# Sample stage of a hybrid trunk: half batches, a finer hand-out, and the pooled inputs ahead of their gates

## The chip, the core and the metric

The kernel runs on one core of one Trainium2 chip. The metric is the device time of one launch in microseconds (us). Before the change it is 2243.91 us, the median of three runs (2242.6 to 2245.94). TensorE is called PE in the rows (its weight loads PEld), VectorE DVE, ScalarE ACT, GpSimd POOL, SyncE SP. All DMAs that bear on the change are issued on SP's queue, which works through them in order.

## The reference

One decoder layer: 1024 prompt tokens and 8 sequences of 4 new tokens (the samples) go through one wide input projection; its columns feed a causal pooling branch and an mLSTM matrix memory; both are gated, merged and projected out. What the change touches, cut to its core:

```python
# pooling branch, group g of 4 (256 columns each), windows 2, 4, 8, 16
pooled = moving_sum(pool_in, win) / cnt - pool_in
a      = (pooled @ pool_w[g]) * pool_scale * silu(pool_z)
# mLSTM memory of the samples: 8 sequences (batches) x 4 heads, state c is 512 x 512
num   = s @ v + g * (q @ c)                   # reads the old state
c_new = decay * c + k.T @ v                   # and writes a new one
```

The old and the new state of the samples are 32 MB each: 32 matrices of 1 MB to read, update and write.

## The kernel before

Everything is float32. A large product is done as three matmuls of a split operand (`mm3`, L376 to L378: high by high, high by low, low by high). `fm` (L429 ff.) computes one 128-column tile of a projection for all 1056 tokens (1024 and 32): 8 steps over the inner dimension by three matmuls, in three chunks of 352 columns (`CW`), or in four of 264 (`CH`) for the pooled inputs.

Work is laid out in stages. The one that matters here runs from about 1357 to 1669 us: `pool_branch` does four groups g, and in each, before the change: PZ, the gate products `pool_z` (two tiles, SiLU on ACT into `sz`); PIN, the pooled inputs (two tiles; each chunk is pooled on DVE and split into `poh` and `pol`, which stand ready as the moving operand); PW, the products with `pool_w` (inner dimension 256, so two steps instead of eight, moving operand `poh`/`pol`), whose result is multiplied into `sz` and stored.

Beside it runs `sample()` (L1044), a Python generator: after each product of eight steps, `fm` calls `tick`, which lets the generator go on to its next `yield`, `RATE_S` = 1.85 steps a product on average. A step is one batch b of one head h. It makes `km` on ACT (L1128), loads the old state as one tile `ct` of 128 x 4 x 512 (1 MB, L1130, three buffers), and then issues on PE four matmuls `num<-ct` (L1132), each 32 wide, that lie on four column groups of the array, and four `kv` products of 512 columns (L1136). On DVE each `kv` is added onto the decayed state in place (L1137). Then `ct` goes out as the new state, 1 MB (L1140). A load can take a buffer only when the store of its tenant three batches before has landed. In the trace each of these four matmuls has two records, so that a whole batch reads `x8` and a half batch `x4`.

The instruction order of each engine comes from the program's order and a list scheduler at build time that keeps a model of time: it moves independent instructions ahead where it sees a wait. So the `num` and `kv` of a batch stand among the matmuls of the gate products and pooled inputs. The weights of each product are loaded by `load_w` (L388 ff., DMA at L397; split at L363 on ACT and L369 on DVE). After this stage come two more groups of merge gates, with the rest of the sample work behind them, then the down projections and the tail.

Of the kernel before, what the change touches and what calls it, by code (L numbers as in the profile page):

```python
# [11 lines left out]
F32R = mybir.dt.float32r  # L12
AF = mybir.ActivationFunctionType
ALU = mybir.AluOpType
# [4 lines left out]
P = 128  # L19
D = 1024  # L20
T = 1024
DB, DS = 8, 4
NS = DB * DS
NT = T + NS
H, DH = 4, 512
M = H * DH
KT = D // P
L = 128
NCH = T // L
CW = NT // 3  # L30
# [7 lines left out]
O_PIN, O_PZ, O_Q, O_K = 0, D, 2 * D, 2 * D + M  # L38
# [5 lines left out]
O_GB = O_GA + D  # L44


RATE_A, RATE_S = 16.0, 1.85
HT = T // 2
SH = NS // 2
HH = HT + SH  # L50
# [3 lines left out]
class Block:  # L54
# [10 lines left out]
    def __init__(self, tr, c0):  # L65
        self.tr, self.c0 = tr, c0
        self.w = {}
        self.saved = {}
        self.raw = [[], []]
        self.begin()  # L70
# [264 lines left out]
class Trunk:  # L335
    def __init__(self, ctx, nc, tc, I, O):
        self.ctx, self.nc, self.tc, self.I, self.O = ctx, nc, tc, I, O
        self.n = 0
        self.bg = None


    def pool(self, name, side="left"):
# [87 lines left out]
    def fm(self, w, f, mov, consume, cw=CW):  # L430

        kt = len(w)
        for j in range(NT // cw):
            ps = self.mmps()
            for k in range(kt):
                wh, wl = w[k][:2]
                mh, ml = mov[k]
                s = slice(j * cw, (j + 1) * cw)
                self.mm3(ps[:, :cw], wh[:, f * P:(f + 1) * P], wl[:, f * P:(f + 1) * P], mh[:, s], ml[:, s],
                         k == 0, k == kt - 1)  # L440
            consume(j, ps)
        if kt == KT:
            self.tick()

    def feed(self, gen, rate):

        self.bg, self.rate, self.acc = gen, rate, 0.0

    def tick(self):
        if self.bg is None:  # L450
            return
        self.acc += self.rate
        while self.acc >= 1.0 and self.bg is not None:
            self.acc -= 1.0
            if next(self.bg, None) is None:
                self.bg = None
# [587 lines left out]
    def sample(self):  # L1044
        nc, I, O = self.nc, self.I, self.O
        a = self.sp
# [3 lines left out]
        ps = self.miscps()  # L1050
        for h in range(H):
            for d in range(4):
                nc.tensor.matmul(ps[32 * h:32 * h + 32, :NS], lhsT=ks[:, h * 4 + d, :], rhs=qs[:, h * 4 + d, :],
                                 start=d == 0, stop=d == 3)
        pb = self.t(a, [P, P], "pb")
        nc.gpsimd.memset(pb, 0.0)
        for h in range(H):
            s = slice(32 * h, 32 * h + 32)
            nc.vector.scalar_tensor_tensor(out=pb[s, s], in0=ps[s, :NS], scalar=KSC, in1=self.DS[s, :], op0=ALU.mult,
                                           op1=ALU.mult)  # L1060
# [3 lines left out]
        ps = self.miscps()  # L1064
# [7 lines left out]
        for h in range(H):  # L1072
            s = slice(h * 4, h * 4 + 4)
# [7 lines left out]
                                    in1=nS[:, :, :, h].unsqueeze(3).to_broadcast([P, 4, DB, DS]), op=ALU.mult)  # L1081
            for d in range(4):
                nc.tensor.matmul(den[32 * h:32 * h + 32, 0:1], lhsT=qn[:, d, :], rhs=self.ones, start=d == 0,
                                 stop=False)
# [10 lines left out]
        ps = self.miscps()  # L1095
# [7 lines left out]
        num = self.t(self.ps, [P, 2, 512], "num")  # L1103
        qm = self.t(a, [P, 132 * DB], "qm")
        nc.gpsimd.memset(qm, 0.0)
        for h in range(H):

            vf = self.t(a, [P, DH], "voz", bufs=3)[:96]
            for g in range(3):
                nc.sync.dma_start(vf[32 * g:32 * g + 32], self.vSD[h])  # L1110
            vst = self.t(a, [96, DH], "vst", F32R, bufs=1)
            self.hi(vst, vf)
            self.lo(vst[64:96], vf[64:96], vst[64:96])
            kst = self.t(a, [96, DH], "kst", F32R, bufs=1)
            ps = self.miscps()
            for d in range(4):
                nc.tensor.transpose(ps[:NS, d * P:(d + 1) * P], ks[:, h * 4 + d, :], self.ident)
            w = self.wcS[:, h:h + 1]
            self.hi(kst[0:32], ps[:NS, :], w)
            self.lo(kst[32:64], ps[:NS, :], kst[0:32], w)  # L1120
            nc.scalar.activation(kst[64:96], kst[0:32].bitcast(F32), AF.Copy)

            nc.vector.tensor_copy(qm.rearrange("p (b r) -> p b r", r=132)[:, :, 0:P]
                                  .rearrange("p b (d x) -> p b d x", d=4)[:, :, :, 0:DS],
                                  qg[:, h * 4:h * 4 + 4].rearrange("p d (b t) -> p b d t", t=DS))
            for b in range(DB):
                km = self.t(a, [96, DH], "km", F32R, bufs=1)
                nc.scalar.activation(km, kst.bitcast(F32), AF.Identity, scale=self.bcol[:96, b:b + 1])  # L1128
                ct = self.t(a, [P, 4, DH], "ct", bufs=3)
                nc.sync.dma_start(ct, I["state_mlstm_C"][b, h].rearrange("(d p) e -> p d e", p=P))  # L1130
                for d in range(4):
                    nc.tensor.matmul(num[32 * d:32 * d + 32, 0, :], lhsT=qm[:, b * P + d * NS:b * P + (d + 1) * NS], rhs=ct[:, d, :],  # L1132
                                     start=b == 0, stop=b == DB - 1)
                for d in range(4):
                    kv = self.t(self.ps, [P, 512], "kv", bufs=2)
                    nc.tensor.matmul(kv, lhsT=km[:, d * P:(d + 1) * P], rhs=vst, start=True, stop=True)  # L1136
                    nc.vector.scalar_tensor_tensor(out=ct[:, d, :], in0=ct[:, d, :],  # L1137
                                                   scalar=self.dec[:, h * DB + b, 1:2], in1=kv,
                                                   op0=ALU.mult, op1=ALU.add)
                nc.sync.dma_start(O["new_C_sample"][b, h].rearrange("(d p) e -> p d e", p=P), ct)  # L1140
                yield True
            nsb = self.t(a, [P, DH], "voz", bufs=3)
            nc.scalar.activation(nsb, num[:, 0, :], AF.Copy)
            nc.tensor.matmul(num[32 * h:32 * h + 32, 1, :], lhsT=self.sel, rhs=nsb, start=True, stop=False)
        vo = []
        for src in (self.vSD, self.oSD, self.zSD):
            x = self.t(a, [P, DH], "voz", bufs=3)
            nc.sync.dma_start(x, src.rearrange("h t e -> (h t) e"))
            vo.append(x)
        nc.tensor.matmul(num[:, 1, :], lhsT=pb, rhs=vo[0], start=False, stop=True)  # L1150
        hc = self.t(a, [P, DH], "shc")
        nc.vector.scalar_tensor_tensor(out=hc, in0=num[:, 1, :], scalar=dn, in1=vo[1], op0=ALU.mult, op1=ALU.mult)
        ss = self.t(a, [P, 1], "sss")
        nc.scalar.activation(vo[1], hc, AF.Square, accum_out=ss)
        r = self.rstd(a, ss, DH)
        nc.vector.scalar_tensor_tensor(out=hc, in0=hc, scalar=r, in1=vo[2], op0=ALU.mult, op1=ALU.mult)
        ps = self.miscps()
        for d in range(4):
            nc.tensor.transpose(ps[:, d * P:(d + 1) * P], hc[:, d * P:(d + 1) * P], self.ident)
# [3 lines left out]
    def pool_branch(self):  # L1163
        nc, I, O = self.nc, self.I, self.O
        a = self.pp
# [6 lines left out]
        for g in range(4):  # L1172
            win = 2 ** (g + 1)
            h1 = self.t(a, [DB * PH, 256], "ph1")
            nc.sync.dma_start(h1, hist[:, g * 256:(g + 1) * 256])
            w = self.load_w(I["w_in"][:, O_PZ + g * 256:O_PZ + (g + 1) * 256], 256)
            sz = []
            for f in range(2):
                z = self.t(a, [P, NT], "sz", bufs=2)

                def ev(j, ps, z=z):
                    s = slice(j * CW, (j + 1) * CW)
                    nc.scalar.activation(z[:, s], ps[:, :CW], AF.Silu)
                self.fm(w, f, self.hmov, ev)
                sz.append(z)
            w = self.load_w(I["w_in"][:, O_PIN + g * 256:O_PIN + (g + 1) * 256], 256)
            pooled = []
            for f in range(2):
# [6 lines left out]
                def ev(j, ps, f=f, ft=ft, ph=ph, pl=pl, prev=prev):  # L1195
# [45 lines left out]
                    self.hi(ph[:, c], po)  # L1241
                    self.lo(pl[:, c], po, ph[:, c])
                self.fm(w, f, self.hmov, ev, CH)
            w = self.load_w(I["pool_w"][g], 256)
            for f in range(2):
                ft = g * 2 + f
# [7 lines left out]
        for f0 in range(0, KT, 4):  # L1254
            ps = self.miscps()
# [4 lines left out]
            s = slice(f0 * P, (f0 + 4) * P)  # L1260
# [251 lines left out]
    def run(self):  # L1512
# [9 lines left out]
        d = self.dp  # L1522
# [57 lines left out]
        def rest():  # L1580
            self.rate = 1.6
            yield from gates
            _a.close()
            self.atp, _at = self.pool("attn", "right")
            self.attn_setup()
            self.rate = RATE_A
            yield from self.attn()
            _at.close()
            self.sp, st = self.pool("sample", "right")
            _s.append(st)  # L1590
            self.rate = RATE_S
            yield from self.sample()
        self.feed(rest(), 1.6)
        self.merge_gates(range(6))
        while not _s:
# [26 lines left out]
        for st in (_l, _f, _w, _c2, _c, _ps):  # L1622
# [4 lines left out]
           state_mlstm_C=(DB, H, DH, DH), state_mlstm_n=(DB, H, DH), state_mlstm_m=(DB, H), p_prompt=(T, PLE),  # L1627
# [20 lines left out]
```

## Time and profile before

| | |
|---|---|
| median of three runs | 2243.91 us |
| the profiled execution | 2243.27 us |
| its span | 2241.5 us (1.77 lie outside it) |
| PE busy in the span | 2154.4 us, 96% |
| DVE, ACT, POOL busy | 57%, 40%, 5% |
| chain that ended last | PE 87%, DMA 6%, DVE 3%, ACT 2% |
| mean granted TensorE clock | 0.986 of 2.4 GHz |

The rows of this kernel are read so: a matmul's length in a timeline includes the pipeline's latency, so the rate is the step from the start of one matmul to the start of the next; an instruction's wait stands in brackets, with the one that ended it. A window row gives a stretch, its length, the busy time and count of PE, PEld, DVE, ACT and POOL, the granted clock as a share of 2.4 GHz, the mean share of 16 DMA engines and GB/s.

### The profile page before, as it was taken

What the parts mean: (1) busy time and instruction counts of PE and PEld (TensorE: products, weight loads), DVE (VectorE), ACT (ScalarE), POOL (GpSimd) and SP (SyncE); (2) the same over time, 40 slices, a digit from 0 to 9 for tenths busy, and PEclk for the clock granted to TensorE, in tenths of its full rate; (3) what the DMA queues carried; (4) which work ended last, traced back from release to release, by engine and by line L of the source; (5) the groups of instructions that cost most, each with busy time, mean ns of one, the idle gap of its engine ahead of it and who ended that gap; (6) DMA issues with size and microseconds to landing.
All of it is one profiled execution on the core that took longest, in us unless ns stands there. A gap on an engine that the chain in (4) does not pass through costs nothing.

```text
span 2241.5 us, 40008 instructions
## 1 busy us (share of the span) xinstructions
PE 2154.4 (96%) x16311; PEld 2045.7 (91%) x16311; DVE 1267.6 (57%) x2184; ACT 903.5 (40%) x1796; POOL 120.2 (5%) x335
## 2 busy tenths in 40 slices
PE   4999999999999999899999899999999999999998
PEld 3899999999999999899999887778778999999998
DVE  7756485556745575536556674575573243543645
ACT  5535454444544453544333342232233331213443
POOL 1100000000100000000000000000000000000000
PEclk8999999999999999999999999999989999999999
DMA  3233323333233321574655645877775343323112
GB/s 129 86 107 120 102 91 110 94 107 116 85 109 110 111 88 41 164 266 143 203 163 177 195 143 168 293 267 252 255 267 171 117 128 110 101 98 111 53 48 83
DMA packets 238600, 312.70 MB, mean 140 GB/s; under 512 B 13994, under 2 KB 170066, under 8 KB 238416
## 3 DMA queue, kind: packets, MB, share of 16 engines
q1 hardware_dynamic: 238416, 310.15, 42.6%
q8 instruction: 128, 2.10, 0.4%
q14 instruction: 56, 0.46, 0.1%
HBM read 200.01 MB, written 110.45 MB: 139 GB/s over the span
## 4 chain that ended last, share of the span: by engine, by line
PE 87%; DMA 6%; DVE 3%; ACT 2%; issue 1%; SPq 1%; POOL 0%; DVEq 0%; POOLq 0%; ACTq 0%
PE mm L215 21%; PE mm L157 15%; PE mm L376 12%; PE mm L378 12%; PE mm L377 12%; PE num L1132 2%; PE misc L917 1%; PE num L376 1%; PE num L377 1%; PE kv L1136 1%; PE num L378 1%; DMA o<-oD 1%; PE kv L376 1%; DMA ct<-state_mlstm_C 1%; PE kv L377 1%; PE kv L378 1%
## 5 line engine op out<-in xcount | busy, mean ns | idle before, releaser
L369 DVE TENSOR_TENSOR wlo<-wraw,whi 128x1024 fp32r<-128x1024 f32 (+1 forms) x220 | 238.4, 1085 | 220.9 <-ACT whi L363 215.5
L363 ACT ACTIVATE whi<-wraw 128x1024 fp32r<-128x1024 f32 (+1 forms) x220 | 209.2, 951 | 348.7 <-PE mm L215 103.4
L376 PE MATMUL mm<-hh,whi 128*128 128x352 f32 (+1 forms) x832 | 264.7, 318 | 12.4 <-ACT sz L1275 6.6
L378 PE MATMUL mm<-hh,wlo 128*128 128x352 f32 (+1 forms) x832 | 262.2, 316 | 0.3 <-DVE wlo L369 0.3
L377 PE MATMUL mm<-hl,whi 128*128 128x352 f32 (+1 forms) x832 | 261.5, 314 | 0.0
L215 PE MATMUL mm<-whi,hl 128*128 128x256 f32 x768 | 216.0, 281 | 0.0
L215 PE MATMUL mm<-wlo,hh 128*128 128x256 f32 x768 | 216.0, 281 | 0.0
L215 PE MATMUL mm<-whi,hh 128*128 128x256 f32 x768 | 214.6, 279 | 0.0
L376 PEld LDWEIGHTS mm<-hh,whi 128*128 128x128 f32 x832 | 158.3, 190 | 25.6 <-ACT sz L1275 8.2
L378 PEld LDWEIGHTS mm<-hh,wlo 128*128 128x128 f32 x832 | 158.2, 190 | 6.8 <-issue 5.0
L377 PEld LDWEIGHTS mm<-hl,whi 128*128 128x128 f32 x832 | 158.7, 191 | 5.7 <-issue 4.4
L157 PE MATMUL mm<-hh,whi 128*128 128x264 f32 x512 | 149.9, 293 | 3.4 <-DVE s L624 2.4
L317 DVE SCALAR_TENSOR_TENSOR z<-z,vcols,z 128x556 f32<-128x556 f32 x192 | 146.7, 793 | 9.5 <-ACT z L315 7.9
L157 PE MATMUL mm<-hl,whi 128*128 128x264 f32 x512 | 147.3, 288 | 0.6 <-DVE hl L371 0.4
L157 PE MATMUL mm<-hh,wlo 128*128 128x264 f32 x512 | 146.7, 286 | 0.0
L215 PEld LDWEIGHTS mm<-whi,hh 128*128 128x128 f32 x768 | 144.7, 188 | 0.0
L215 PEld LDWEIGHTS mm<-whi,hl 128*128 128x128 f32 x768 | 144.6, 188 | 0.0
L215 PEld LDWEIGHTS mm<-wlo,hh 128*128 128x128 f32 x768 | 144.3, 188 | 0.2
L1137 DVE SCALAR_TENSOR_TENSOR ct<-ct,dec,kv 128x512 f32<-128x512 f32 x128 | 93.2, 742 | 73.9 <-PE kv L1136 67.0
L378 PE MATMUL mm<-mvhB,wlo 128*128 128x352 f32 x384 | 123.0, 322 | 0.0
L377 PE MATMUL mm<-mvlB,whi 128*128 128x352 f32 x384 | 122.7, 321 | 0.0
L376 PE MATMUL mm<-mvhB,whi 128*128 128x352 f32 x384 | 121.6, 323 | 0.0
(438 smaller groups left out, 6060.2 us busy)
## 6 DMA issues: line engine op xcount, KB each, us to landing
wraw<-w_in SPq DMA_DIRECT2D x112, 512.0 KB
ct<-state_mlstm_C SPq DMA_DIRECT2D x32, 1024.0 KB
new_C_sample<-ct SPq DMA_DIRECT2D x32, 1024.0 KB
qkD<-z SPq DMA_DIRECT2D x64, 256.0 KB
qk<-qkD SPq DMA_DIRECT2D x16, 1024.0 KB
sgD<-sz SPq DMA_DIRECT2D x16, 528.0 KB
sg<-sgD SPq DMA_DIRECT2D x16, 528.0 KB
vD<-z SPq DMA_DIRECT2D x32, 256.0 KB
```

Source lines behind the costliest of these rows:

```text
L157: self.tr.nc.tensor.matmul(ps[:, j, :CH], lhsT=st[:, k], rhs=mv[k][:, c], start=start and k == 0 and n == 0, stop=stop and k == 3 and n == ...
L215: self.tr.nc.tensor.matmul(ps[:, t // 2, t % 2 * 256:t % 2 * 256 + 256], lhsT=st[k][:, c], rhs=mv[:, k], start=start and t % 2 == 0 and k ...
L317: nc.vector.scalar_tensor_tensor(out=acc, in0=z[:, o:o + tot], scalar=wc(o), in1=acc, op0=ALU.mult, op1=ALU.add)
L363: self.nc.scalar.activation(out, in_, AF.Copy)
L369: self.nc.vector.tensor_tensor(out=out, in0=in_, in1=hi.bitcast(F32), op=ALU.subtract)
L376: mm(ps, lhsT=sh, rhs=mh, start=start, stop=False)
L377: mm(ps, lhsT=sh, rhs=ml, start=False, stop=False)
L378: mm(ps, lhsT=sl, rhs=mh, start=False, stop=stop)
L917: nc.tensor.matmul(out, lhsT=qk[:, 4 + d, i * L:(i + 1) * L], rhs=qk[:, d, i * L:], start=d == 0, stop=d == 3)
L1132: nc.tensor.matmul(num[32 * d:32 * d + 32, 0, :], lhsT=qm[:, b * P + d * NS:b * P + (d + 1) * NS], rhs=ct[:, d, :], start=b == 0, stop=b = ...
L1136: nc.tensor.matmul(kv, lhsT=km[:, d * P:(d + 1) * P], rhs=vst, start=True, stop=True)
L1137: nc.vector.scalar_tensor_tensor(out=ct[:, d, :], in0=ct[:, d, :], scalar=self.dec[:, h * DB + b, 1:2], in1=kv, op0=ALU.mult, op1=ALU.add)
```

## The change

The memory of a batch is held as two half tiles of 128 x 2 x 512 (512 KB), seven buffers instead of three of 1 MB; each half has its own load, its own store and its own `yield`, so that `sample()` has 64 steps in the batches instead of 32 and three more near its end. `RATE_S` doubles, and in this stage `tick` is called after every chunk of a product with the chunk's share of the rate (a third, or a quarter) instead of once a product. `km` has two buffers. In `pool_branch`, the products PIN with the pooling stand ahead of PZ.

```diff
-RATE_A, RATE_S = 16.0, 1.85
+RATE_A, RATE_S = 16.0, 3.7
@@ fm
             consume(j, ps)
-        if kt == KT:
-            self.tick()
+            if kt == KT and self.fine:
+                self.tick(cw / NT)
+        if kt == KT and not self.fine:
+            self.tick(1.0)
@@ feed, tick
-        self.bg, self.rate, self.acc = gen, rate, 0.0
+        self.bg, self.rate, self.acc, self.fine = gen, rate, 0.0, False
-        self.acc += self.rate
+        self.acc += self.rate * part
@@ sample
-                km = self.t(a, [96, DH], "km", F32R, bufs=1)
+                km = self.t(a, [96, DH], "km", F32R, bufs=2)
                 nc.scalar.activation(km, kst.bitcast(F32), AF.Identity, scale=self.bcol[:96, b:b + 1])
-                ct = self.t(a, [P, 4, DH], "ct", bufs=3)
-                nc.sync.dma_start(ct, I["state_mlstm_C"][b, h].rearrange("(d p) e -> p d e", p=P))
+                ct = []
+                for i in range(2):
+                    c = self.t(a, [P, 2, DH], "ct", bufs=7)
+                    nc.sync.dma_start(c, I["state_mlstm_C"][b, h, i * 2 * P:(i + 1) * 2 * P]
+                                      .rearrange("(d p) e -> p d e", p=P))
+                    ct.append(c)
                 for d in range(4):
-                    nc.tensor.matmul(num[32 * d:32 * d + 32, 0, :], lhsT=qm[...], rhs=ct[:, d, :],
-                                     start=b == 0, stop=b == DB - 1)
-                for d in range(4):
-                    kv = self.t(self.ps, [P, 512], "kv", bufs=2)
...
-                nc.sync.dma_start(O["new_C_sample"][b, h].rearrange("(d p) e -> p d e", p=P), ct)
-                yield True
+                    nc.tensor.matmul(num[32 * d:32 * d + 32, 0, :], lhsT=qm[...],
+                                     rhs=ct[d // 2][:, d % 2], start=b == 0, stop=b == DB - 1)
+                for i, c in enumerate(ct):
+                    for d in range(2):
+                        kv = self.t(self.ps, [P, 512], "kv", bufs=2)
...
+                    nc.sync.dma_start(O["new_C_sample"][b, h, i * 2 * P:(i + 1) * 2 * P]
+                                      .rearrange("(d p) e -> p d e", p=P), c)
+                    yield True
@@ pool_branch, each group
             nc.sync.dma_start(h1, hist[:, g * 256:(g + 1) * 256])
-            w = self.load_w(I["w_in"][:, O_PZ + ...], 256)       # PZ: sz, ten lines
...
             w = self.load_w(I["w_in"][:, O_PIN + ...], 256)
...
                 self.fm(w, f, self.hmov, ev, CH)
+            w = self.load_w(I["w_in"][:, O_PZ + ...], 256)       # the same ten lines
...
             w = self.load_w(I["pool_w"][g], 256)
@@ run, rest
-            self.rate = RATE_S
+            self.rate, self.fine = RATE_S, True
```

What the instruction order makes of it, at three places. The numbers behind a name are buffer numbers; lines of the changed file lie from 1 to 13 below those of before (`num` L1132 there is L1139, `kv` L1136 is L1144, the load L1130 is L1135, the store L1140 is L1149, `mm3` L377 to L379).

PE before, in the second half of the stage: a batch among the pooled inputs' products.

```order
L378 MATMUL mm_16533<-hh_135,wlo_16405 128x264
L376 MATMUL mm_16533<-hh_135,whi_16410 128x264
L1132 MATMUL num_15377<-ct_16383,qm_15378 32x512 x4
L377 MATMUL mm_16533<-hl_136,whi_16410 128x264
L378 MATMUL mm_16533<-hh_135,wlo_16411 128x264
L376 MATMUL mm_16533<-hh_135,whi_16410 128x264
L1136 MATMUL kv_16374<-vst_16226,km_16360 128x512
L377 MATMUL mm_16533<-hl_136,whi_16410 128x264
L378 MATMUL mm_16533<-hh_135,wlo_16411 128x264
```

PE after, early in the stage: a batch whose two halves lie apart, among gate products.

```order
L1144 MATMUL kv_15776<-vst_15384,km_15763 128x512
L1139 MATMUL num_15377<-ct_15945,qm_15378 32x512 x2
L1144 MATMUL kv_15821<-vst_15384,km_15763 128x512
L377 MATMUL mm_15968<-hh_135,whi_15830 128x352
L378 MATMUL mm_15968<-hl_136,whi_15830 128x352
L379 MATMUL mm_15968<-hh_135,wlo_15831 128x352
L377 MATMUL mm_15968<-hh_135,whi_15830 128x352
L378 MATMUL mm_15968<-hl_136,whi_15830 128x352
L379 MATMUL mm_15968<-hh_135,wlo_15831 128x352
L1139 MATMUL num_15377<-ct_15947,qm_15378 32x512 x2
```

The four `num` products of a batch stood together; now the two of each half stand with other matmuls between them in many places. Over the whole order, the `num` products form 40 uninterrupted runs before and 53 after; one of the 53 holds the products of two batches, seven in all. The number of `num` and `kv` products is the same, 128 each.

SP before, at the start of the stage: the DMA queue's stores and loads.

```order
L1140 DMA new_C_sample<-ct_15399 128x4x512
L1130 DMA ct_15647<-state_mlstm_C 128x4x512
L1140 DMA new_C_sample<-ct_15526 128x4x512
L1130 DMA ct_15834<-state_mlstm_C 128x4x512
L1140 DMA new_C_sample<-ct_15626 128x4x512
L1130 DMA ct_15855<-state_mlstm_C 128x4x512
L1140 DMA new_C_sample<-ct_15647 128x4x512
```

SP after, at the same place.

```order
L1149 DMA new_C_sample<-ct_15399 128x2x512
L1135 DMA ct_15767<-state_mlstm_C 128x2x512
L1188 DMA ph_2143_16143<-state_pool 120x256
L1149 DMA new_C_sample<-ct_15401 128x2x512
L1135 DMA ct_15869<-state_mlstm_C 128x2x512
L1149 DMA new_C_sample<-ct_15563 128x2x512
L398 DMA wraw_16145<-w_in 128x4x256
L1135 DMA ct_15871<-state_mlstm_C 128x2x512
L398 DMA wraw_16151<-w_in 128x4x256
L1149 DMA new_C_sample<-ct_15565 128x2x512
L1149 DMA new_C_sample<-ct_15667 128x2x512
L1135 DMA ct_15945<-state_mlstm_C 128x2x512
```

Each load stands behind the store that frees its buffer, as before; there are twice as many pairs, each of half the size, and SP issues 817 DMAs in all instead of 751.

PE before, where the last group's pooled inputs end.

```order
L377 MATMUL mm_18243<-hl_136,whi_17888 128x264
L378 MATMUL mm_18243<-hh_135,wlo_17889 128x264
L1209 MATMUL misc_18271<-ident_112,ph_2405_17625 128x120
L1132 MATMUL num_15377<-ct_18292,qm_15378 32x512 x4
L1257 MATMUL misc_18388<-ident_112,np_2022_15430 47x128 x2
L376 MATMUL mm_18338<-poh_17892,whi_18334 128x352
L377 MATMUL mm_18338<-pol_17893,whi_18334 128x352
L378 MATMUL mm_18338<-poh_17892,wlo_18335 128x352
```

PE after, where the last group's gate products end.

```order
L378 MATMUL mm_18372<-hl_136,whi_18164 128x352
L379 MATMUL mm_18372<-hh_135,wlo_18165 128x352
L1144 MATMUL kv_18368<-vst_17917,km_18322 128x512
L1139 MATMUL num_15377<-ct_18400,qm_15378 32x512 x2
L1139 MATMUL num_15377<-ct_18402,qm_15378 32x512 x2
L377 MATMUL mm_18428<-poh_17701,whi_18424 128x352
L378 MATMUL mm_18428<-pol_17702,whi_18424 128x352
L379 MATMUL mm_18428<-poh_17701,wlo_18425 128x352
```

Before, the products with `pool_w` follow straight on the last pooled inputs that they read; after, the 144 matmuls of the gate products stand between. From the merge gates behind this stage on, PE's order is the same (3602 rows).

## Rows read from the trace of the kernel before

**Rows 1.** Windows: stretch, length, busy us per engine, clock, DMA share, GB/s.

```profile
1357.40:1669.40 312.00, 299.48 (x1903) 240.51 (x1904) 190.99 (x393) 87.11 (x173) 14.95 (x55) 0.97 0.72 252
1360.00:1371.00 11.00, 8.47 (x54) 5.19 (x52) 4.03 (x17) 1.10 (x2) 0.00 (x0) 0.84 0.88 304
1415.00:1427.00 12.00, 10.19 (x59) 6.49 (x57) 10.81 (x22) 2.27 (x6) 0.33 (x2) 1.00 1.04 366
1490.00:1502.00 12.00, 9.85 (x54) 6.21 (x53) 8.58 (x16) 3.43 (x7) 1.52 (x3) 0.86 0.73 263
1570.00:1580.00 10.00, 7.99 (x46) 5.76 (x45) 9.46 (x20) 2.18 (x4) 0.30 (x2) 1.00 0.87 316
1645.20:1669.40 24.20, 20.35 (x87) 12.32 (x86) 18.97 (x38) 6.22 (x12) 0.59 (x3) 0.72 0.75 241
```

**Rows 2.** Groups on PE in 1357.4 to 1669.4: count, busy, mean ns, idle before.

```profile
L376 PE MATMUL mm<-hh,whi 128*128 128x264 f32 x256 | 73.7, 288 | 0.0
...
L376 PE MATMUL mm<-hh,whi 128*128 128x352 f32 x177 | 58.2, 329 | 1.0 <-ACT sz L1183 1.0
...
L1136 PE MATMUL kv<-vst,km 96*128 96x512 f32 x126 | 51.1, 435 | 1.7 <-ACT km L1128 1.0 <-DVE ct L1137 0.5
L1132 PE MATMUL num<-ct,qm 128*32 128x512 f32 x248 | 43.9, 647 | 9.7 <-DMA ct<-state_mlstm_C 7.2 <-DVE nn L1089 2.5
L376 PE MATMUL mm<-poh,whi 128*128 128x352 f32 x48 | 17.6, 379 | 0.8 <-DVE sz L1250 0.3 <-ACT poh L363 0.3
```

**Rows 3.** Timeline of PE: start, length, instruction; a product of 512 among 264.

```profile
1386.34 0.40 PE L1136 MATMUL kv<-vst,km 96*128 96x512 f32 x1
1386.58 0.29 PE L376 MATMUL mm<-hh,whi 128*128 128x264 f32 x1
1386.70 0.28 PE L377 MATMUL mm<-hl,whi 128*128 128x264 f32 x1
```

**Rows 4.** Timeline of PE: a whole batch of num between products.

```profile
1383.00 0.32 PE L377 MATMUL mm<-hl,whi 128*128 128x352 f32 x1
1383.16 0.32 PE L378 MATMUL mm<-hh,wlo 128*128 128x352 f32 x1
1383.41 1.07 PE L1132 MATMUL num<-ct,qm 128*32 128x512 f32 x8
1384.41 0.39 PE L376 MATMUL mm<-hh,whi 128*128 128x264 f32 x1
1384.64 0.28 PE L377 MATMUL mm<-hl,whi 128*128 128x264 f32 x1
```

**Rows 5.** Timeline of PE: num that waited (bracket: idle before, its releaser).

```profile
1497.00 1.93 PE L1132 MATMUL num<-ct,qm 128*32 128x512 f32 x8 [2.13 <-DMA ct<-state_mlstm_C]
...
1658.80 1.93 PE L1132 MATMUL num<-ct,qm 128*32 128x512 f32 x8 [2.58 <-DMA ct<-state_mlstm_C]
```

**Rows 6.** Chain of waits, in time: start, length, piece.

```profile
1359.08 1.95 DMA voz<-vSD
...
1413.42 4.65 DMA new_C_sample<-ct
1418.10 7.28 DMA ct<-state_mlstm_C
...
1445.88 0.98 PE num L1132 x4
...
1739.64 4.23 DMA draw<-hcD
```

**Rows 7.** Waits of the DMA queue SP, 1350 to 1700: sum, times, longest.

```profile
SPq L1130 <- DMA new_C_sample<-ct: 94.1, 26, 6.1
...
SPq L397 <- DVE wlo L369: 19.6, 14, 5.6
```

**Rows 8.** Timeline of the queue SP: a store and the load behind it.

```profile
1388.40 0.38 SPq L1140 DMA_DIRECT2D new_C_sample<-ct  x1
1392.95 0.37 SPq L1130 DMA_DIRECT2D ct<-state_mlstm_C  x1
```

More of the change, by code (lines that the diff above doesn't have):

```diff
@@ L339, in __init__ @@
         self.bg = None
+        self.fine = False
     def pool(self, name, side="left"):
@@ L441, in fm, with tick @@
             consume(j, ps)
-        if kt == KT:
-            self.tick()
+            if kt == KT and self.fine:
+                self.tick(cw / NT)
+        if kt == KT and not self.fine:
+            self.tick(1.0)
     def feed(self, gen, rate):
-        self.bg, self.rate, self.acc = gen, rate, 0.0
-    def tick(self):
+        self.bg, self.rate, self.acc, self.fine = gen, rate, 0.0, False
+    def tick(self, part):
         if self.bg is None:
             return
-        self.acc += self.rate
+        self.acc += self.rate * part
         while self.acc >= 1.0 and self.bg is not None:
@@ L1126, in sample @@
             for b in range(DB):
-                km = self.t(a, [96, DH], "km", F32R, bufs=1)
+                km = self.t(a, [96, DH], "km", F32R, bufs=2)
                 nc.scalar.activation(km, kst.bitcast(F32), AF.Identity, scale=self.bcol[:96, b:b + 1])
-                ct = self.t(a, [P, 4, DH], "ct", bufs=3)
-                nc.sync.dma_start(ct, I["state_mlstm_C"][b, h].rearrange("(d p) e -> p d e", p=P))
-                for d in range(4):
-                    nc.tensor.matmul(num[32 * d:32 * d + 32, 0, :], lhsT=qm[:, b * P + d * NS:b * P + (d + 1) * NS], rhs=ct[:, d, :],
-                                     start=b == 0, stop=b == DB - 1)
@@ L1134, in sample @@
-                for d in range(4):
-                    kv = self.t(self.ps, [P, 512], "kv", bufs=2)
[L1136 to L1139, printed above, removed]
-                nc.sync.dma_start(O["new_C_sample"][b, h].rearrange("(d p) e -> p d e", p=P), ct)
@@ L1141, in sample @@
-                yield True
+                ct = []
[4 more added lines that the diff above has]
+                    ct.append(c)
+                for d in range(4):
+                    nc.tensor.matmul(num[32 * d:32 * d + 32, 0, :], lhsT=qm[:, b * P + d * NS:b * P + (d + 1) * NS],
+                                     rhs=ct[d // 2][:, d % 2], start=b == 0, stop=b == DB - 1)
@@ new lines, in sample @@
+                for i, c in enumerate(ct):
+                    for d in range(2):
+                        kv = self.t(self.ps, [P, 512], "kv", bufs=2)
+                        nc.tensor.matmul(kv, lhsT=km[:, (2 * i + d) * P:(2 * i + d + 1) * P], rhs=vst, start=True,
+                                         stop=True)
+                        nc.vector.scalar_tensor_tensor(out=c[:, d], in0=c[:, d],
+                                                       scalar=self.dec[:, h * DB + b, 1:2], in1=kv,
+                                                       op0=ALU.mult, op1=ALU.add)
+                    nc.sync.dma_start(O["new_C_sample"][b, h, i * 2 * P:(i + 1) * 2 * P]
+                                      .rearrange("(d p) e -> p d e", p=P), c)
+                    yield True
@@ L1149, in sample @@
             vo.append(x)
+        yield True
         nc.tensor.matmul(num[:, 1, :], lhsT=pb, rhs=vo[0], start=False, stop=True)
@@ L1152, in sample @@
         nc.vector.scalar_tensor_tensor(out=hc, in0=num[:, 1, :], scalar=dn, in1=vo[1], op0=ALU.mult, op1=ALU.mult)
+        yield True
         ss = self.t(a, [P, 1], "sss")
@@ L1156, in sample @@
         nc.vector.scalar_tensor_tensor(out=hc, in0=hc, scalar=r, in1=vo[2], op0=ALU.mult, op1=ALU.mult)
+        yield True
         ps = self.miscps()
@@ L1175, in pool_branch @@
             nc.sync.dma_start(h1, hist[:, g * 256:(g + 1) * 256])
[L1176 to L1185, printed above, removed]
             w = self.load_w(I["w_in"][:, O_PIN + g * 256:O_PIN + (g + 1) * 256], 256)
@@ L1243, in pool_branch, with ev @@
                 self.fm(w, f, self.hmov, ev, CH)
+            w = self.load_w(I["w_in"][:, O_PZ + g * 256:O_PZ + (g + 1) * 256], 256)
+            sz = []
+            for f in range(2):
+                z = self.t(a, [P, NT], "sz", bufs=2)
+                def ev(j, ps, z=z):
+                    s = slice(j * CW, (j + 1) * CW)
+                    nc.scalar.activation(z[:, s], ps[:, :CW], AF.Silu)
+                self.fm(w, f, self.hmov, ev)
+                sz.append(z)
             w = self.load_w(I["pool_w"][g], 256)
```

## The prediction

> **What bounds the kernel now.** I read the page first: PE is busy for 96% of the span and carries the chain that ended last, so time can come only from PE's own work, from its clock, or from the few per cent in which it waits. Then I read windows, because the change touches one stage. That stage lasts 312.0 us, from 1357.4 to 1669.4, and PE is busy for 299.5 of them, DVE for 191, with the DMA engines at a share of 0.72 and 252 GB/s [rows 1]. PE's order behind it is the same after the change, so the stage is the whole case.
>
> How much of the 312 is work? Rates are steps between starts. A matmul of 264 columns takes 0.12 us and one of 512 (`kv`) 0.24 [rows 3]; one of 352 takes 0.16, and a batch's four `num` products take 1.00 together, with 0.23 instead of 0.12 until the second matmul behind them, so 1.11 for the run [rows 4]. Counts: 256 x 3 of 264 columns, (177 + 176 + 176) of the gates and 48 x 3 = 144 of `pool_w` at 352, 126 `kv`, and 248 records of `num`, which are 31 batches [rows 2]; these stand in 39 runs there (40 in the whole order). So 768 x 0.12 = 92.2, 673 x 0.16 = 107.7, 126 x 0.24 = 30.2, 39 x 1.11 = 43.3, and about 8 (an estimate) for small transposes and selections: 281. The other 31 us are loss.
>
> Where are they? Five windows hold 22.6 of them [rows 1]. Idle: 11 - 8.47 = 2.5 at the stage's start, 1.8 at 1415, 2.15 at 1490, 2.0 at 1570, 3.85 at the end, together 12.3; that is nearly all idle time of the stage (312.0 - 299.5 = 12.5). Clock: the granted clock is 0.84, 0.86 and 0.72 in three of them, so PE ran part of the time at 1.2 GHz, the lower level, after it had idled; that costs 0.16 x 11 + 0.14 x 12 + 0.28 x 24.2 = 10.3. A batch of `num` that waited 2.13 or 2.58 us for its state and then took 1.93 instead of 1.07 shows both at once [rows 5]. The chain says what these waits are: store of a state tile 4.65 us, and behind it the load into the same buffer 7.28 us [rows 6]; with three buffers the load cannot start before the store three batches back has landed, and the queue itself stands 94.1 us at such loads [rows 7]. The remaining 8.4 us are scattered.
>
> **The change part by part.**
>
> Split `num` products. They run four side by side on column groups. Two of them cost as much as four: a run of `x4`, half a batch, is 0.98 us on PE [rows 6], against 1.00 for the whole [rows 4]. The order after the change has 53 runs, of which one is long enough for two passes, so 54 passes instead of 40. Cost: 14 x (1.00 + 0.11) = 15.5 us. The bounds: at nothing for the 0.11, 14 x 0.98 = 13.7; and below, if the halves that stand near each other still overlap, 0, which the `x4` row speaks against, as it was measured in just such a place. I take 15.5. The `kv` products may be cut into more pieces at no cost, since a single one among other matmuls already goes at its 0.24 [rows 3].
>
> Halves and seven buffers. A buffer is freed and filled again in smaller pieces. In the order before, the shortest distances of PE work from a tile's last `kv` to the first `num` of its next tenant are (by the rates above) 8.0, 9.4, 9.8 and 10.2 us, and then 11.6; just those four waited, so the refill needs about 4.65 + 7.28 = 11.9 [rows 6]. After, the four shortest are 8.4, 9.2, 9.7 and 10.0, the next 11.1, the median 17.3 against 14.4. So the distances grow little; what counts is how long half a refill takes. The trace has no 512 KB state transfer. Bounds: no saving, 11.9, which would leave four waits of 1.9 to 3.5 us; half, 6.0, no wait. Between lie a 512 KB load with 4.23 us and a 64 KB one (`voz`, a copy of V's rows) with 1.95 [rows 6]; a line from 64 KB at 1.95 to 1 MB at 4.65 passes 512 KB at 3.2. Store and load together are then 6.4 to 8.5, and 9.7 with something for the crowd on the DMA engines (1.04 share at 1415, [rows 1]). I take 9, so waits of 0 to 0.6 and some 1.2 us in the middle three places, where 5.95 idle + 1.7 clock = 7.7 stood.
>
> Finer ticks, twice the rate. The pace of the sample work is the same, its grain is finer: 0.93 to 1.23 steps a chunk. This costs nothing on PE beyond the split above. At the start the first batch still waits for the stage's first load (idle 2.5, clock 1.8); I keep 2.5 of this 4.3, as a half tile lands sooner.
>
> PIN ahead of PZ. No instruction is added; the DMAs of two weight loads change places on SP's queue. The `pool_w` products get 144 x 0.16 = 23 us of gate products between them and the DVE pooling that they read. The end of the stage, where idle 3.85 and clock 6.8 stand, is relieved: I keep 2 of these 10.65. What this uncovers is the `sz` buffers of the next group, which are read by the `pool_w` products and stored before the next PZ; the next PIN now lies between, so they are free in time. `km` with two buffers takes out the 1.0 us that `kv` waited for `km`; `sz` waits 1.0 at the stage's first gate product, and `pool_w` 0.8 on DVE and ACT [rows 2]. With their surroundings I take 3 of the 8.4 scattered and 1.0 for the first gate product. Bounds for the two together: 0 and 9.4.
>
> Sum: of 22.6, kept 2.5 + 1.2 + 2 = 5.7, so won 16.9, + 3 + 1.0 = 20.9, less 15.5: 5.4 faster. Against the profiled execution of 2243.27 (0.64 below the median) that is 2237.9, so **2238 us**.
>
> **The rivals.**
>
> B, no difference. The waits are halved and not removed, because the distances grow so little: of 16.9 won only 8.5, + 4 - 15.5 = 3 slower, 2246. For it: the shortest distance after the change, 8.4, is no longer than 8.0 before. Against it: the median grows by 3 us.
>
> C, slower: the queue SP becomes the bound. One DMA queue in order, and behind each store the load that needs its buffer: before, a store issued at 1388.40 holds the load until 1392.95, so 4.55, + 0.37 for the load [rows 8]. If a half's store lands in 4.23 like the 512 KB row [rows 6], 64 pairs need 64 x (4.23 + 0.37) = 294; some 60 other transfers of the stage at 0.37 add 22, and half of the 19.6 us in which the queue waits for weight buffers [rows 7] add 10: 326 against a stage of 312 - 5 = 307. Then the time is 2238 + 19 = 2257. It decides from a landing of (307 - 32) / 64 - 0.37 = 3.9 us on. At 3.2 the same sum is 64 x 3.57 + 32 = 260, and the queue is not the bound. For it: the only 512 KB row. Against it: the 1.95 of the small one, and that the DMA engines are not full.
>
> The Trainium skill bears on this in "DMA: Bandwidth & Descriptors", section "Anatomy of one DMA": in its fit a transfer pays about 2.0 us of fixed time and its bytes at 436 GB/s on top, so halving a transfer halves only the second part. It is a rule that speaks against this change, fitted to another queue's path than SP's. By it 1 MB takes 4.4 (the trace: 4.65) and 512 KB 3.2 (the trace has 4.23 for another tensor); two halves 6.4 where one whole was 4.4. By the fit C would stay away, and by the row it would come.
>
> D, faster by more: two halves run at another price than the `x4` row, or mostly overlap, so that splitting costs next to nothing: 2243.3 - 20.9 = 2222. For it nothing but the lack of a row with two products of different halves a few matmuls apart.
>
> **How the numbers follow.** Forecast 0.55, with its own range of 2230 to 2246: the lower end with 9.4 instead of 4.0 for the scattered loss and 13.7 for the split, the upper one with 5 us more of waits left and none of the scattered won. B 0.18, C 0.17, D 0.10. The range over all is 2224 to 2254: it takes in B, most of D and the milder half of C. A measurement here can tell 0.2%, some 4.5 us, from no change; so faster means below 2239.4 and slower above 2248.4. Of the forecast's 0.55 some 0.40 lie below 2239.4, with D's 0.10: 0.50. Same: 0.15 of the forecast and 0.12 of B: 0.27. Slower: C's 0.17 and 0.06 of B: 0.23.
>
> **What would show it.** After the change, `num` in the timeline as `x4` near 0.98 each and more PE time in its group, if the first term is right; a run of them below 0.7 refutes it. Around 1415, 1490 and 1570 no wait on `ct` and a granted clock of 1.00; PE waits on `ct` in every group instead would speak for B, or, with SP's store-to-load steps above 4.3 us and the stage near 325, for C. `pool_w` products that wait for DVE would refute the term of the order. The stage should last about 307 us. The prediction is wrong as a whole if the stage changes by less than 2 us or grows.

## The result, and the profile after

The change makes the kernel slower: 2260.81 us (median of four runs, 2257.83 to 2263.29) against 2244.77 for the kernel before in the same rounds, a ratio of 1.0073 with a 95% interval of 1.0058 to 1.0088. The profiled execution took 2263.29 us, 20.0 more than the one before the change. Most of the time is lost in the one stage that the change edits: the last `pool_w` product starts 15.7 us later than before (1684.9 against 1669.2), and from there to PE's last matmul it takes 567.6 us instead of 563.3.

The windows of PE in the changed kernel (columns as in [rows 1]) show the stage from its first product to the end of its last, and three stretches with waits:

```profile
1357.20:1685.30 328.10, 313.54 (x1908) 245.74 (x1909) 192.21 (x387) 88.22 (x176) 13.81 (x55) 0.97 0.72 240
1425.00:1437.00 12.00, 8.72 (x39) 5.73 (x39) 5.98 (x8) 3.68 (x5) 0.00 (x0) 0.88 0.70 227
1592.00:1604.00 12.00, 9.36 (x49) 6.00 (x48) 8.42 (x13) 3.42 (x5) 0.00 (x0) 0.89 1.02 354
1655.00:1680.00 25.00, 19.48 (x100) 13.33 (x98) 8.40 (x11) 5.45 (x8) 0.00 (x0) 0.86 0.69 207
```

The stage takes 328.1 us instead of 312.0. PE is busy for 14 us more, and idle for 14.6 instead of 12.5: the idle time that was to go is still there. It has moved, and the granted clock is low again, 0.86 to 0.89 of 2.4 GHz in these three stretches. They hold 11.4 us of idle time and 6.3 of lost clock (one less the granted share, times the length). The groups on PE (the answer to [rows 2]):

```profile
L1139 PE MATMUL num<-ct,qm 128*32 128x512 f32 x256 | 59.0, 623 | 12.8 <-DMA ct<-state_mlstm_C 12.7
L1144 PE MATMUL kv<-vst,km 96*128 96x512 f32 x122 | 50.2, 422 | 1.2 <-DVE ct L1146 1.2
```

`num` costs 59.0 us for 256 records; before it was 43.9 for 248, so 45.3 for 256. The 13.7 more are 14 passes at 0.98. Its wait for `ct` is 12.7 us, where before it was 7.2 and 2.5 behind the start's small work.

The chain of waits (start, length, piece) shows the end of the last group. Before the change a store and the load behind it stood in the chain once, at 1413 [rows 6]; now stores follow each other, each released by the load issue between them:

```profile
1651.31 5.04 DMA new_C_sample<-ct
1656.38 0.38 SPq L1135
1656.85 4.96 DMA new_C_sample<-ct
1661.87 0.38 SPq L1135
1662.34 5.07 DMA new_C_sample<-ct
1667.43 0.38 SPq L1135
1667.87 5.00 DMA new_C_sample<-ct
1672.88 3.94 DMA ct<-state_mlstm_C
```

This is a lock step of the DMA queue. A store lands after 5.0 us, only then the load behind it is issued (0.38), and at once the next store, which is long due; the load has only 0.45 us to itself before the store is in flight beside it. One half takes 5.5 us, so a batch 11. Before, the stores of three batches were issued at 1388.40, 1396.79 and 1404.79, about 8.2 us a batch. PE is busy for about 9.8 us a batch (313.5 / 32): the queue kept ahead of PE then, and now is slower than PE wherever the lock step holds. That is so in stretches and not throughout: PE waits for `ct` six times, 12.7 us in all. SP's timeline has 857 DMAs against 793 before the change (not 817 against 751): 32 more loads and 32 more stores. SP's timeline shows what a half costs otherwise; first a store with no load issued in the 17 us before it, then one 0.47 us behind a load:

```profile
1379.58 0.38 SPq L1149 DMA_DIRECT2D new_C_sample<-ct  x1
1382.37 0.38 SPq L1135 DMA_DIRECT2D ct<-state_mlstm_C  x1
```

```profile
1650.84 0.38 SPq L1135 DMA_DIRECT2D ct<-state_mlstm_C  x1
1651.31 0.42 SPq L1149 DMA_DIRECT2D new_C_sample<-ct  x1
1656.38 0.38 SPq L1135 DMA_DIRECT2D ct<-state_mlstm_C  x1
```

Alone, a half has landed after 2.79 us (1379.58 to 1382.37), behind a load after 5.07. Of the 39 places in the changed kernel where a load comes right behind a store, 22 have another load less than 1.5 us ahead of the store; in 15 of these the trace names that store as what ended the load's wait, at a median of 5.06 us. That is more than the 4.2 us that the stores of a whole megabyte at 1396.79 and 1404.79 took in the kernel before, where the last load had been issued 3.8 us ahead.

### The profile page after: what moved, and what is told of

Its sections match the earlier page's. It is cut to its first block, busy times and chain, and to the rows that moved or that the text cites. A ratio compares the mean times of both kernels' runs of the same rounds, so it can differ in the third digit from the quotient of the medians.

```text
span 2261.6 us, 40109 instructions
## 1 busy us (share of the span) xinstructions
PE 2169.4 (96%) x16311; PEld 2052.4 (91%) x16311; DVE 1271.7 (56%) x2184; ACT 903.1 (40%) x1796; POOL 119.3 (5%) x335
## 4 chain that ended last, share of the span: by engine, by line
PE 87%; DMA 6%; DVE 3%; ACT 2%; issue 1%; SPq 0%; POOL 0%; DVEq 0%; POOLq 0%; ACTq 0%
PE mm L215 21%; PE mm L157 14%; PE mm L377 12%; PE mm L378 12%; PE mm L379 12%; DMA new_C_sample<-ct 2%; PE num L1139 2%; PE misc L920 2%; PE num L377 1%; PE num L378 1%; PE num L379 1%; PE kv L377 1%; PE kv L1144 1%; PE kv L378 1%; PE kv L379 1%; PE misc L703 1%
## 5 line engine op out<-in xcount | busy, mean ns | idle before, releaser
L377 PE MATMUL mm<-hh,whi 128*128 128x352 f32 (+1 forms) x832 | 266.1, 320 | 14.1 <-ACT sz L1288 8.7
L379 PE MATMUL mm<-hh,wlo 128*128 128x352 f32 (+1 forms) x832 | 262.7, 316 | 2.1 <-DVE wlo L370 2.1
L377 PEld LDWEIGHTS mm<-hh,whi 128*128 128x128 f32 x832 | 159.5, 192 | 32.9 <-ACT sz L1288 11.0
L379 PEld LDWEIGHTS mm<-hh,wlo 128*128 128x128 f32 x832 | 159.6, 192 | 5.4 <-DVE wlo L370 2.4
L379 PE MATMUL mm<-mvhB,wlo 128*128 128x352 f32 x384 | 123.3, 322 | 0.0
L377 PE MATMUL mm<-mvhB,whi 128*128 128x352 f32 x384 | 122.4, 325 | 0.2
```

Source lines behind the costliest of these rows:

```text
L377: mm(ps, lhsT=sh, rhs=mh, start=start, stop=False)
L379: mm(ps, lhsT=sl, rhs=mh, start=False, stop=stop)
```

## The experiments

Two theories were to be told apart. **Split:** a pass of `num` costs the same whether it holds two products or four, and the half tiles make more passes. **Queue:** the halves put twice as many store and load pairs into SP's queue, each of which holds up the one behind it. The rivals: the new order of the pooled inputs, the finer hand-out, the second `km` buffer. All ratios are against the kernel before on the same chip, with 95% intervals; a pass is an uninterrupted run of up to four `num` products on PE, and passes are counted in the instruction order.

**Order alone.** The kernel before with the block of the gate products (PZ) put behind that of the pooled inputs (PIN).

```diff
-            w = self.load_w(I["w_in"][:, O_PZ + ...], 256)      # PZ, ahead of PIN
...
+            w = self.load_w(I["w_in"][:, O_PZ + ...], 256)      # PZ, behind PIN
```

> The kernel before with one edit, the pooled inputs ahead of the gates; whole 1 MB tiles, 40 passes of num. If the loss of the change lies in the halves (queue or split), this one has none of it and wins the waits at the stage's end: 2236 to 2242 us. If the new order itself costs time (pooled inputs meeting the first batches, weight loads in other places), it is slower than before: 2248 or more.

0.9996 (0.9983 to 1.0009): no difference, so neither a win nor a loss of the order alone shows. `num` waits 4.8 us for `ct`, against 7.2 before.

**Halves alone.** The kernel before with half tiles in seven buffers, one step a batch.

```diff
-                ct = self.t(a, [P, 4, DH], "ct", bufs=3)
+                for i in range(2):
+                    c = self.t(a, [P, 2, DH], "ct", bufs=7)
...
```

> The kernel before with the two half tiles, seven buffers, and nothing else: one step a batch, a tick a product, the old order. 48 passes of num instead of 40. Theory queue and split together: a half's store still takes about 5 us to land and its load stands behind it, and 8 passes add 8 to 9 us: 2252 to 2262. Theory split alone (halves refill faster than whole tiles, waits go): 2244 + 9 - 10 = 2243. Theory queue alone (splitting free): 2246 to 2252, with the waits of num on ct at 10 us or more.

1.0089 (1.0076 to 1.0103), as slow as the whole change, without the new order, the finer hand-out and the second `km` buffer. PE's waits (sum, times, longest):

```profile
PE num L1136 <- DMA ct<-state_mlstm_C: 19.2, 13, 2.6
```

The waits did not go, which speaks against the split alone, and the time is above what the queue alone was to cost. So with 8 passes more, both losses are there.

**Whole tiles.** All of the change but the halves and the finer hand-out. The edit is shown against the changed kernel.

```diff
-RATE_A, RATE_S = 16.0, 3.7
+RATE_A, RATE_S = 16.0, 1.85
@@ fm
-            if kt == KT and self.fine:
-                self.tick(cw / NT)
-        if kt == KT and not self.fine:
-            self.tick(1.0)
+        if kt == KT:
+            self.tick()
@@ sample
-                    c = self.t(a, [P, 2, DH], "ct", bufs=7)
...
+                ct = self.t(a, [P, 4, DH], "ct", bufs=3)
```

> The changed kernel with whole 1 MB tiles in three buffers again and a rate of 1.85, so that a step is a batch; fine ticks, two km buffers and the new order stay. 38 passes of num. If the halves are what costs: 2232 to 2242. If the finer hand-out or the order costs, it stays above 2250.

0.9950 (0.9934 to 0.9965), 2232.31 us: faster than both kernels. PE's waits:

```profile
PE num L1132 <- DMA ct<-state_mlstm_C: 1.3, 2, 0.8
```

The expectation counts the finer hand-out (the fine ticks) among what stays, but this run's kernel calls `tick` once a product, like the kernel before. So it takes out the halves and the finer hand-out together, and what it has beyond the kernel before is the new order with two `km` buffers. No run has whole tiles with the finer hand-out, and its part is not shown here: in the instruction order it makes a difference, 41 passes of `num` instead of 38. That the halves cost without it, the run before this one shows.

**Stores on GpSimd's queue.** The changed kernel with one word changed.

```diff
-                    nc.sync.dma_start(O["new_C_sample"][b, h, i * 2 * P:(i + 1) * 2 * P]
+                    nc.gpsimd.dma_start(O["new_C_sample"][b, h, i * 2 * P:(i + 1) * 2 * P]
```

> The changed kernel with the half stores issued on GpSimd's queue, so that no store stands behind a load that waits; 60 passes of num by the scheduler's order, 6 more than the changed kernel. Theory queue: the 12.7 us of waits of num on ct and the low clock behind them (about 4) go: with the 6 passes (6 us) 2250 us. Theory split alone: nothing gained, 2261 + 6 = 2267. If a split costs nothing: 2242 or less.

1.0034 (1.0022 to 1.0047). The waits are all but gone, and the six more passes (60) stand in PE's groups:

```profile
PE num L1139 <- DMA ct<-state_mlstm_C: 2.0, 2, 1.1
```

```profile
L1139 PE MATMUL num<-ct,qm 128*32 128x512 f32 x256 | 63.4, 604 | 2.1 <-DMA ct<-state_mlstm_C 2.0
```

**Joined, and joined with stores on GpSimd's queue.** The changed kernel with the products of a batch in another sequence, which leaves 44 passes; then the same with the edit of the run before, 42 passes.

```diff
-                for d in range(4):
+                for d in (2, 0, 3, 1):
                     nc.tensor.matmul(num[32 * d:32 * d + 32, 0, :], ...
```

> The changed kernel with the four num products of a batch issued in the order 2, 0, 3, 1 (each needs the same data as before), after which the scheduler leaves them apart less often: 44 passes instead of 54, with half tiles, stores and queue as in the changed kernel. Theory split, a pass at 1.0 to 1.1 us whatever it holds: 10 to 11 us less, 2250. Theory queue alone: PE then waits as long as before or longer, 2258 to 2262.

> The same with the half stores on GpSimd's queue too: 42 passes, 18 fewer than with the stores there alone (2250.9). If the two losses are separate and add up: 2250.9 - 18 x 1.05 = 2232. If PE, once it has fewer passes, runs into the transfers again: 2238 or more.

Joined alone: 1.0062 (1.0044 to 1.0081), not to be told from the change. Busy time of `num` falls from 59.0 to 48.3 us, but much of what the saved passes win comes back as waits, 18.9 us instead of 12.7:

```profile
PE num L1139 <- DMA ct<-state_mlstm_C: 18.9, 8, 7.0
```

With the stores out of SP's queue: 0.9950 (0.9937 to 0.9964), 2232.61 us. Between the two runs with the stores there, 18 passes make 1.0034 - 0.9950 = 0.84%, 18.9 us, 1.05 each. Its waits and its `num`:

```profile
PE num L1139 <- DMA ct<-state_mlstm_C: 2.0, 3, 1.2
```

```profile
L1139 PE MATMUL num<-ct,qm 128*32 128x512 f32 x256 | 44.2, 604 | 2.4 <-DMA ct<-state_mlstm_C 2.0 <-DVE ksum L1089 0.4
```

The two joined runs differ by the queue of the stores and two passes: 1.0062 - 0.9950 = 1.1%, some 25 us, of which 16.9 are the waits. On GpSimd's queue the half stores land no sooner than in the lock step, after 5.1 us at the median (last column: from issue to landing):

```profile
new_C_sample<-ct POOLq DMA_DIRECT2D x64, 512.0 KB, 5.1
```

So it is not by the store's own length that PE came to wait, but by stores and loads that hold each other up in one queue.

**Half loads.** The run with whole tiles, each loaded by two DMAs and stored by one.

```diff
-                nc.sync.dma_start(ct, I["state_mlstm_C"][b, h].rearrange("(d p) e -> p d e", p=P))
+                for i in range(2):
+                    nc.sync.dma_start(ct[:, i * 2:i * 2 + 2], I["state_mlstm_C"][b, h, i * 2 * P:(i + 1) * 2 * P]
+                                      .rearrange("(d p) e -> p d e", p=P))
```

> The kernel with whole 1 MB tiles, new order and two km buffers (2232.3), with each tile loaded by two DMAs of 512 KB and stored by one of 1 MB: 60 passes of num instead of 38, and no more stores than before. Theory split: 22 passes at 1.0 to 1.1, 2254 to 2256. If what costs is the number of stores alone: 2232 to 2236.

1.0060 (1.0046 to 1.0073). `num` here (last column: idle before) never waits, and nearly all the loss is its own time. First the run with whole tiles, then this one:

```profile
L1132 PE MATMUL num<-ct,qm 128*32 128x512 f32 x256 | 41.1, 604 | 1.3 <-DMA ct<-state_mlstm_C 1.3
L1134 PE MATMUL num<-ct,qm 128*32 128x512 f32 x256 | 63.8, 604 | 0.0
```

1.0060 - 0.9950 = 1.1%, 24.7 us for 22 passes, 1.12 each; by busy time it is 22.7 us, 1.03 each. The intervals leave 4 to 5 us either way on such a difference of two runs, and the busy time agrees within that.

**Half stores.** The run with whole tiles, each stored by two DMAs.

```diff
-                nc.sync.dma_start(O["new_C_sample"][b, h].rearrange("(d p) e -> p d e", p=P), ct)
+                for i in range(2):
+                    nc.sync.dma_start(O["new_C_sample"][b, h, i * 2 * P:(i + 1) * 2 * P]
+                                      .rearrange("(d p) e -> p d e", p=P), ct[:, i * 2:i * 2 + 2])
```

> The kernel with whole 1 MB tiles, new order and two km buffers (2232.3), with each tile loaded by one DMA of 1 MB and stored by two of 512 KB: 38 passes, so no split of num at all. If more stores on SP's queue cost by themselves: 2238 or more, with more than the 1.3 us of waits of num on ct. If the queue only costs when each half's load stands behind its own store: 2230 to 2235.

0.9985 (0.9976 to 0.9995): 0.35%, about 8 us, above whole tiles, without a single pass more:

```profile
PE num L1132 <- DMA ct<-state_mlstm_C: 7.1, 5, 2.4
```

More stores cost by themselves. Whether through the queue, or because a buffer is freed only when both of its stores have landed, this run does not tell apart.

**The second `km` buffer alone; whole tiles with the stores on GpSimd's queue.** The kernel before with two `km` buffers; the same with the stores moved (the second edit); and the order alone with the stores moved.

```diff
-                km = self.t(a, [96, DH], "km", F32R, bufs=1)
+                km = self.t(a, [96, DH], "km", F32R, bufs=2)
...
-                nc.sync.dma_start(O["new_C_sample"][b, h].rearrange("(d p) e -> p d e", p=P), ct)
+                nc.gpsimd.dma_start(O["new_C_sample"][b, h].rearrange("(d p) e -> p d e", p=P), ct)
```

> The kernel before with two km buffers and nothing else: 38 passes. Of the 11 us that whole tiles with new order and two km buffers won, the order alone has shown nothing measurable. If km makes it: 2232 to 2236. If it takes both together: 2240 to 2244. By the 1.0 us that kv waited for km before, 2243.

> The kernel before with two km buffers, the old order, and the stores on GpSimd's queue: 36 passes. If the loss of the second km buffer alone (2252, waits of num on ct 15.6 us) lies in SP's queue: the waits go, and with the clock behind them 2252 - 16 - 4 = 2232 to 2238. If it lies elsewhere: 2248 or more.

> The kernel before with whole tiles and one km buffer, the new order, and the 1 MB stores on GpSimd's queue: 37 passes of num. If it is the stores in SP's queue that make PE wait (6.9 us on num with the order alone): waits below 2 us and 2241 - 3 - 5 = 2233, the fastest so far or level with whole_tiles. If the order alone is limited by something else: 2240.

1.0035 (1.0017 to 1.0052; nine runs from 2245.66 to 2261.99 us), 1.0063 (1.0047 to 1.0078) and 0.9986 (0.9972 to 0.9999). The first went against all that was expected of it; the other two came out where their expectations put it if SP's queue is not what limits. PE's waits in the first two:

```profile
PE num L1132 <- DMA ct<-state_mlstm_C: 15.6, 9, 4.6
```

```profile
PE num L1132 <- DMA ct<-state_mlstm_C: 17.8, 9, 5.4
```

With whole tiles, moving the stores to another queue does not take the waits away (8.1 us of them also stand in the order with moved stores). There are only three buffers then, and a load has to wait for the store of its own buffer in any queue; with the halves there are seven, and there moving the stores did take the waits away. That the three buffers are the limit is an argument: no run gave whole tiles a fourth. Why the second `km` buffer loses alone and wins together with the new order is not settled: the waits of `num` on `ct` go with it (7.2 us before, 4.8 with the order, 15.6 with `km`, 1.3 with both), but what in the sequence of loads and stores makes them was not tried one by one.

## Why the prediction was wrong

It said 5.4 us faster; the change is 16 us slower by the medians. By its steps:

- Split, 15.5 us: right. Busy time of `num` rose by 13.7, and the runs price a pass at 1.03 to 1.12 against the forecast's 1.11. The rule that two products cost as much as four was in [rows 6] and held.
- The gain, 20.9 us: this is the step that failed, in its term on halves and seven buffers. By the prediction's own rates the stage after the change has 720 x 0.12 + 720 x 0.16 + 122 x 0.24 + 54 x 1.11 + 8 = 299 us of work, so 29 us of loss where 31 were before: 2 us won, not 20.9. The three stretches shown above alone hold 17.7 of the 29; the forecast had 5.7 left of the 22.6 in its five windows. I took 9 us for the refill of a half and asked only whether that fits between a tile's last use and its next. The 3.2 us on the line were if anything too long for a lone half, which lands in 2.79. But in a queue where each load stands behind a store, a half's store is issued right behind its predecessor's load, and there it takes 5.0; and the load behind it waits all that time.
- Rival C was the right mechanism, with a place (SP's queue), a condition (a landing above 3.9 us) and a price (2257) that came within 4 us of the result. That the price came so near is in part luck: it lets the queue bound the whole stage, 64 pairs at 4.60 us, while the trace has 39 places with a load right behind a store, many of them shorter, and PE waiting in six places. I gave it 0.17, because I set the small transfer's 1.95 against its 4.23. What I should have read is the distance of a load from the next store before the change, 3.84 us (1392.95 to 1396.79): neither of the two stores that I used, at 1388.40 and 1413.42, had a load issued in the 3 us ahead of it. That holds only as long as the queue waits for PE and DVE, and not they for the queue. By the Trainium skill's fit ("DMA: Bandwidth & Descriptors", section "Anatomy of one DMA — SWDGE (gpsimd) path"), which is for GpSimd's path, such a half takes an estimated 3.2 us; the trace shows 2.79 on SP's queue for one alone and 5.07 behind a load, so the fit did not decide it.
- The price of the split and the waits were treated as a sum. They are partly one under the other: when the passes were cut from 54 to 44, the waits grew from 12.7 to 18.9 us, and the time did not change beyond its interval; with the stores out of SP's queue each pass counted in full.
- Order, ticks, `km`: the finer hand-out was not tried by itself. The last joined run has it and is as fast (0.9950) as whole tiles without it, so no loss by it shows there. The end of the stage was not relieved by 8.65 us: 5.5 of idle time and 3.5 of clock stand from 1655 to 1680, behind the lock step that begins at 1645. The wait that stood there before the change did not come from a store alone, either. Its load was issued 6.95 us behind the store of its buffer (1645.31), and the chain of before has a weight load of 5.16 us (from 1646.45) ahead of its 6.49 us. The order with `km` wins 0.5% with whole tiles. With the halves no run sets it apart: 1.0089 without the two and the finer hand-out, 1.0073 with all three.
- Behind the stage 4.3 us were lost, of which the prediction had nothing; what lost them was not followed up.

## What to carry to other kernels

Before you cut a transfer in pieces, work out what the in-order queue needs for one unit of work, with the load in flight ahead of each store, and compare it with the pace of the bound engine; a duration read from a transfer with no load close ahead of it is not the duration in a full queue. Products that share one pass of the array on column groups are to be kept together: whatever makes half of their operands ready earlier takes them apart, at the price of a pass. Where two limits lie close together, mending one can show little: fewer passes alone gave 1.0062 and the stores moved alone 1.0034, against 1.0073 for the change, and only the run with both mended (0.9950) tells what each is worth.

## What the runs showed of the hardware

Two 32-wide products on two of four column groups cost PE about the same as four, 1.03 to 1.12 us a pass over 18 and 22 passes. And stores took longer with a load issued just ahead of them: 2.79 us for 512 KB alone and 5.07 behind a load of 512 KB. For 1 MB it was 4.20 with a load 3.84 us ahead in the kernel before, and 8.13 with one 0.88 us ahead in the run with whole tiles (6.42 and 10.16 in its two other places with a load less than 2 us ahead):

```profile
1396.72 0.37 SPq L1130 DMA_DIRECT2D ct<-state_mlstm_C  x1
1397.60 0.38 SPq L1140 DMA_DIRECT2D new_C_sample<-ct  x1
1405.73 0.37 SPq L1130 DMA_DIRECT2D ct<-state_mlstm_C  x1
```
